# Output weights' low parts pinned on GpSimd, a tanh in a PSUM bank and a small square on ScalarE, in the mixer of a two-layer decoder trunk

## The chip, the cores and the metric

The kernel runs on one core of a Trainium2 chip. A core has five engines that each work through their own list of instructions in order and meet only at semaphores: TensorE (PE in the profile; its weight loads are PEld), VectorE (DVE), ScalarE (ACT), GpSimd (POOL) and SyncE (SP), which here only issues DMAs. [...]

The metric is device time in microseconds for one execution. Before the change it is 1792.57 us, the median of 3 runs (1792.52 to 1795.35).

## The reference

Two layers, each a feed-forward block, a mixer and a second feed-forward block, on x of 512 positions by 1024 features. The change touches the mixer alone:

```python
h = rms_norm(x, mix_norm[l])
a, g, q, k, v = jnp.split(h @ w_in[l], splits, axis=-1)
conv_out = conv_module(a, g, conv_w[l], conv_b[l], conv_norm[l])
...
diff_out = diff_attention(q, k, v, rel_bias, lam, lam_init, subln_norm[l])
x = x + jnp.concatenate([conv_out, diff_out], axis=-1) @ w_out[l]

def conv_module(a, g, conv_w, conv_b, conv_norm):
    u = a * jax.nn.sigmoid(g)
    y = lax.conv_general_dilated(u, rhs, ...) + conv_b      # causal, depthwise, 31 taps
    return jax.nn.silu(rms_norm(y, conv_norm))              # norm over the 512 channels
```

diff_attention has four heads. Each has two softmax maps, A1 - lambda * A2 weighs the values, and the result gets an RMS norm per head.

## The kernel before

All products of weights are made in three matmuls: a float32 weight or activation is split into a high part (a rounding copy, written by ScalarE at L100) and a low part (the difference, L101, by VectorE or GpSimd), and high x high, high x low and low x high are summed in PSUM (`mm3`, L172, L175, L176). `chunk` loads 128 x 1024 weights over the SP queue into one of 5 raw buffers and makes the two parts in one of 4 buffers each. Features stand on partitions and positions on the free axis.

The mixer of a layer goes so. The input projection gives gated conv channels u (4 tiles of 128 channels), then keys, queries and values. `attend(n)` runs a software pipeline over 16 steps, a step being one head of one block of 128 queries, blocks in the order 3, 2, 1, 0: scores on TensorE (L717, two float32 matmuls into banks "sc" and "po"), bias added on VectorE (L721), exp on ScalarE (L725), the two maps joined on VectorE (L728, L730, L731), transposed by TensorE (L738), copied by ScalarE (L740), and multiplied with the values (L747). After a block's fourth head its norm is taken: the squared sums of the exps `se` (L754, VectorE, 128 x 4), squares on ScalarE (L756), a reduction (L758), sum and power on GpSimd (L759, L223), the scaling (L762), a transpose (L774) and the split into high and low parts (L776, L777). Conv and attention write their parts into `acth` and `actl`, conv into feature tiles 0 to 3.

The conv module runs beside attention. Channel tile 0 has its 31 taps on ScalarE and GpSimd (products `prod`, L671, sums `yp`, L672), tiles 1 and 2 on VectorE (L686), tile 3 has 10 taps on the first pair and 21 on VectorE, joined at L689. Squares (L655, L658) are summed on GpSimd (`csum`, L659). `conv_finish` turns them into 1/rms per position: transposes (L230), a reduction and a scaling on VectorE (L234, L235), the power on GpSimd (L223), transposes back (L243) and a copy to `rb` (L247). Then, for each channel tile, GpSimd multiplies with rb (L697), ScalarE takes a tanh into an SBUF buffer of which there is one (L699), VectorE makes (tanh + 1) * z (L700), ScalarE the high part (L701) and VectorE the low part from z and the high part (L702).

The output projection takes the conv half first (`half` 0, all positions, 8 output tiles of 12 matmuls of 512 columns), then the attention half for positions 256 to 511 and 0 to 255 (256 columns). Each pair of output tiles uses one chunk of `wout`, with the low part on GpSimd. Its banks are the score banks "sc" and "po"; VectorE adds each tile to x (L828).

The order of instructions on each engine is made by a scheduler from the program and the estimates it has, except where `keep_in_program_order` pins an instruction against those written before and after it. So the first four chunks of `wout`, written after attention, are in fact loaded early, and their low parts stand among GpSimd's last conv taps.

Of the kernel before, what the change touches and what calls it, by code (L numbers as in the profile page):

```python
# [11 lines left out]
F32 = mybir.dt.float32  # L12
F32R = mybir.dt.float32r
I32 = mybir.dt.int32
AF = mybir.ActivationFunctionType
# [3 lines left out]
P = 128  # L19
DEPTH = 2  # L20
SEQ = 512
# [46 lines left out]
def trunk(ctx: ExitStack, tc: tile.TileContext, xt, par, lamv, relb, onehot,  # L68
# [12 lines left out]
    def f32(ap):  # L81
        return ap.bitcast(F32)
# [3 lines left out]
    def bank(tag, name):  # L86
        return psum.tile([P, 512], F32, tag=tag, name=name, bufs=BANKS[tag])
# [5 lines left out]
        dt = F32 if "raw" in tag else F32R  # L93
        return wp.tile([P, n], dt, tag=tag, name=tag, bufs=RING[tag])

    def parts_of(raw, hi, lo, eng=None, first=False):
        if first:
            V.tensor_scalar(hi, raw, 1.0, None, op0=ALU.mult)
        else:
            S.activation(hi, raw, AF.Copy)  # L100
        (eng or V).tensor_tensor(out=lo, in0=raw, in1=f32(hi), op=ALU.subtract)  # L101

    def chunk(src, eng=None):
        raw, hi, lo = ring("wraw"), ring("whi"), ring("wlo")
        nc.sync.dma_start(raw, src)
        parts_of(raw, hi, lo, eng)
        return hi, lo

    def by_halves(src):
# [435 lines left out]
    def mixer(l, pr, after):  # L545
        with tc.tile_pool(name="mix", bufs=1) as mp, tc.tile_pool(name="mt", bufs=2) as mt:
# [111 lines left out]
                    S.activation(sq, y, AF.Square)  # L658
                    G.tensor_tensor(csum, csum, sq, op=ALU.add)  # L659

            def conv_taps(c, n):

                wc = _AT["conv_w"] + c * TAPS
                yp = None
                if n:
                    yp = mp.tile([P, SEQ], F32, tag="yp%d" % (n < TAPS), name="yp")
                    G.tensor_scalar(yp, us[c][:, 0:SEQ], pars[l][:, wc : wc + 1], col(l, "conv_b", c),
                                    op0=ALU.mult, op1=ALU.add)
                    for t in range(1, n):
                        p = mt.tile([P, SEQ], F32, tag="prod", name="prod")  # L670
                        S.activation(p, us[c][:, t : t + SEQ], AF.Copy, scale=pars[l][:, wc + t : wc + t + 1])  # L671
                        G.tensor_tensor(yp, yp, p, op=ALU.add)  # L672
                if n == TAPS:
                    ys[c] = yp
                    conv_square(c, yp)
                    return
                y = bank("y", "ps_y")
                if not n:
                    V.tensor_scalar(y, us[c][:, 0:SEQ], pars[l][:, wc : wc + 1], col(l, "conv_b", c),
                                    op0=ALU.mult, op1=ALU.add)  # L680
                else:
                    V.tensor_scalar(y, us[c][:, n : n + SEQ], pars[l][:, wc + n : wc + n + 1], None, op0=ALU.mult)

                ys[c] = us[c][:, PAD:]
                for t in range(n + 1 if n else 1, TAPS):
                    V.scalar_tensor_tensor(ys[c] if t == PAD and not n else y, us[c][:, t : t + SEQ],  # L686
                                           pars[l][:, wc + t : wc + t + 1], y, op0=ALU.mult, op1=ALU.add)
                if n:
                    V.tensor_tensor(ys[c], y, yp, op=ALU.add)  # L689
                conv_square(c, ys[c])  # L690

            def conv_finish():
                rcv = spread(rows_rstd(csum, CC, "c")[0], "rb")
                for c in range(CT):
                    z = ys[c]
                    hg = ghalf[l][:, c : c + 1]
                    G.tensor_tensor(z, z, rcv, op=ALU.mult)  # L697
                    th = mt.tile([P, SEQ], F32, tag="gl", name="th", bufs=1)
                    S.activation(th, z, AF.Tanh, scale=hg)  # L699
                    V.scalar_tensor_tensor(z, th, 1.0, z, op0=ALU.add, op1=ALU.mult)  # L700
                    S.activation(ch[:, c, :], z, AF.Copy, scale=hg)  # L701
                    V.scalar_tensor_tensor(cl[:, c, :], z, hg, f32(ch[:, c, :]), op0=ALU.mult, op1=ALU.subtract)  # L702
# [40 lines left out]
            def values(i, h):  # L743
                if h == 0:
                    pos[i] = bank("mm", "ps_o")
                for j in range(i + 1):
                    T.matmul(pos[i][:, h * VD : (h + 1) * VD], ats[i, h][:, j * P : (j + 1) * P], vv[:, j, h, :],  # L747
                             start=j == 0, stop=j == i)
                if h < HEADS - 1:
                    return  # L750
                po = pos[i]

                se = small.tile([P, HEADS], F32, tag="se", name="se")
                V.scalar_tensor_tensor(se, sums[i][:, 0, :], VD * EPS, sums[i][:, 0, :], op0=ALU.mult, op1=ALU.mult)  # L754
                sq = tmp.tile([P, SEQ], F32, tag="sq", name="sq")
                S.activation(sq, po, AF.Square)  # L756
                so = small.tile([P, HEADS], F32, tag="so", name="so")
                V.tensor_reduce(so, sq.rearrange("p (h d) -> p h d", h=HEADS), axis=AX.X, op=ALU.add)  # L758
                G.tensor_tensor(so, so, se, op=ALU.add)  # L759
                ro = rsqrt(so, HEADS)  # L760
                ov = mt.tile([P, HEADS, VD], F32, tag="ov", name="ov")
                V.tensor_tensor(  # L762
                    ov, po.rearrange("p (h d) -> p h d", h=HEADS),
                    ro.unsqueeze(2).broadcast_to([P, HEADS, VD]), op=ALU.mult,
                )
                outs[i] = ov
# [39 lines left out]
            for n in range(2):  # L806
                attend(n)
                project_values(NT - 1 - 2 * n)
                project_values(NT - 2 - 2 * n)
            for c in range(CT):  # L810
                conv_taps(c, POOL_TAPS[c])
            for n in range(2, len(steps) + 5):
                attend(n)
            conv_finish()

            for half, t in ((0, slice(0, SEQ)), (1, slice(SEQ // 2, SEQ)), (1, slice(0, SEQ // 2))):
                if t.stop == SEQ:
                    w = [None] * 4  # L820
                for m in range(KT):
                    if w[m // 2] is None:
                        w[m // 2] = chunk(wout[l, half, m // 2], G)
                    ps = bank(("sc", "po")[m % 2], "ps_out")[:, : t.stop - t.start]
                    for kk in range(4):
                        k = half * 4 + kk
                        mm3(ps, wpart(w[m // 2], (m % 2) * 4 + kk), (ch[:, k, t], cl[:, k, t]), kk == 0, kk == 3)
                    V.tensor_tensor(x[:, m, t], ps, x[:, m, t], op=ALU.add)  # L828

                    if half == 1 and t.start == 0 and m < KT // 2:  # L830
                        after(m)
# [12 lines left out]
    for l in range(DEPTH):  # L844
        nxt = {}

        def then(l2, gain):
            def after(m):
                if m == 0:
                    nxt["p"] = Prep(l2, gain)  # L850
                nxt["p"].tile(m)
            return after
# [82 lines left out]
```

## Time and profile before

| What | Value |
|---|---|
| median of 3 runs | 1792.57 us (1792.52 to 1795.35) |
| the profiled execution | 1792.75 us, of which 1791.0 us are its span |
| granted TensorE clock | 1.000 |
| mixer tail of layer 0 (last value projections to the next feed-forward block) | about 471 to 551 us of the span |
| the same of layer 1 | about 889.5 us later |

A page of the profile gives the busy time of each engine and the chain of waits that ended last. A timeline row is: start, duration (us), engine, line, operation, output and inputs, shapes, count; in brackets the idle time before it and what ended that. Rows that merge several instructions give the time from the first's start to the last's end. A group row has the line, operation, shapes and count, then busy us and mean ns, then idle time before. Matmuls overlap, so the issue interval, not the duration, is what one costs.

### The profile page before, as it was taken

How to read it: one execution, taken by the hardware profiler on the slowest of the kernel's cores; microseconds unless marked ns; L12 is line 12 of the kernel's file. 1: busy time of each engine (PE TensorE's matmuls, PEld its weight loads, DVE VectorE, ACT ScalarE, POOL GpSimd, SP SyncE). 2: the span in 40 equal slices, each digit the busy share in tenths (PEclk: the TensorE clock that was granted, in tenths of full speed). 3: DMA queues.
4: the chain of work that ended last, by engine and by line, in shares of the span. 5: the costliest groups of instructions: out<-in, count | busy, mean ns of one | idle time of the engine just before them, and what ended most of it. 6: DMA issues, size and time to landing. Idle time of an engine off the chain costs nothing.

```text
span 1791.0 us, 28372 instructions
## 1 busy us (share of the span) xinstructions
PE 1783.5 (100%) x10861; PEld 1591.8 (89%) x10861; DVE 1203.1 (67%) x1849; ACT 895.0 (50%) x1479; POOL 643.1 (36%) x453
## 2 busy tenths in 40 slices
PE   9999999999999999999999999999999999999999
PEld 7899899888788899899888998998887888998997
DVE  7877476568867767477566665765788587674762
ACT  6455265445845455265433643654558354552651
POOL 2242232269843133133102412312798331322420
PEclk9999999999999999999999999999999999999999
DMA  7366466322212367367333654663231133664651
GB/s 247 107 174 185 112 179 175 119 93 94 71 48 84 94 165 191 104 171 193 102 95 99 169 168 121 174 182 118 71 116 50 48 107 96 169 172 112 182 150 59
DMA packets 111721, 231.24 MB, mean 129 GB/s; under 512 B 12151, under 2 KB 33414, under 8 KB 111584
## 3 DMA queue, kind: packets, MB, share of 16 engines
q1 hardware_dynamic: 91488, 191.93, 33.5%
q0 software_dynamic: 19808, 37.33, 12.5%
q8 instruction: 85, 1.39, 0.3%
q14 instruction: 52, 0.43, 0.1%
q10 hardware_dynamic: 288, 0.16, 0.0%
HBM read 227.26 MB, written 3.42 MB: 129 GB/s over the span
## 4 chain that ended last, share of the span: by engine, by line
PE 95%; DVE 4%; DMA 0%; issue 0%; ACT 0%; SPq 0%; DVEq 0%; ACTq 0%
PE ps_pair L384 38%; PE ps_d L172 9%; PE ps_d L176 9%; PE ps_d L175 9%; PE ps_pair L176 5%; PE ps_pair L175 5%; PE ps_pair L172 5%; PE ps_pair L601 2%; PE ps_pair L600 2%; PE ps_pair L602 2%; PE ps_out L175 1%; PE ps_out L176 1%; PE ps_out L172 1%; PE ps_sc L717 1%; DVE actl L261 1%; PE ps_v L632 1%
## 5 line engine op out<-in xcount | busy, mean ns | idle before, releaser
L100 ACT ACTIVATE whi<-wraw 128x512 fp32r<-128x512 f32 (+2 forms) x600 | 466.0, 801 | 611.3 <-PE ps_pair L384 226.4
L101 DVE TENSOR_TENSOR wlo<-wraw,whi 128x512 fp32r<-128x512 f32 (+2 forms) x557 | 521.6, 959 | 219.6 <-ACT whi L100 214.6
L384 PE MATMUL ps_pair<-acth,wlo 128*128 128x256 f32 x1088 | 308.3, 283 | 0.0
L384 PE MATMUL ps_pair<-actl,whi 128*128 128x256 f32 x1088 | 308.3, 283 | 0.0
L384 PE MATMUL ps_pair<-acth,whi 128*128 128x256 f32 x1088 | 308.3, 283 | 0.0
L175 PE MATMUL ps_d<-hl,whi 128*128 128x512 f32 x704 | 274.3, 390 | 0.0
L176 PE MATMUL ps_d<-hh,wlo 128*128 128x512 f32 x704 | 273.1, 389 | 0.0
L172 PE MATMUL ps_d<-hh,whi 128*128 128x512 f32 x704 | 269.3, 390 | 0.0
L384 PE MATMUL ps_pair<-th,wlo 128*128 128x256 f32 x816 | 231.2, 283 | 0.0
L384 PE MATMUL ps_pair<-tl,whi 128*128 128x256 f32 x816 | 231.1, 283 | 0.0
L384 PE MATMUL ps_pair<-th,whi 128*128 128x256 f32 x816 | 231.1, 283 | 0.0
L150 POOL DMA_DIRECT2D wraw<-in_gu x68 | 81.9, 1204 | 412.9 <-DMA wraw<-in_gu 143.2
L155 POOL TENSOR_TENSOR wraw<-wraw 128x512 f32<-128x512 f32 x68 | 104.9, 1543 | 331.0 <-DMA wraw<-in_gu 239.8
L384 PEld LDWEIGHTS ps_pair<-acth,whi 128*128 128x128 f32 x1088 | 209.1, 192 | 0.3
L384 PEld LDWEIGHTS ps_pair<-actl,whi 128*128 128x128 f32 x1088 | 209.1, 192 | 0.3
L384 PEld LDWEIGHTS ps_pair<-acth,wlo 128*128 128x128 f32 x1088 | 209.1, 192 | 0.0
L484 DVE SCALAR_TENSOR_TENSOR x<-ps_d,x 128x512 f32<-128x512 f32 x96 | 64.8, 689 | 179.0 <-PE ps_d L176 178.7
L175 PE MATMUL ps_pair<-actl,whi 128*128 128x512 f32 x448 | 175.0, 391 | 0.3 <-DVE actl L261 0.2
L176 PE MATMUL ps_pair<-acth,wlo 128*128 128x512 f32 x448 | 174.6, 391 | 0.0
L172 PE MATMUL ps_pair<-acth,whi 128*128 128x512 f32 x448 | 174.0, 393 | 0.2 <-ACT whi L100 0.2
L384 PEld LDWEIGHTS ps_pair<-th,whi 128*128 128x128 f32 x816 | 156.7, 192 | 0.6
L384 PEld LDWEIGHTS ps_pair<-tl,whi 128*128 128x128 f32 x816 | 156.7, 192 | 0.7
(169 smaller groups left out, 3247.1 us busy)
## 6 DMA issues: line engine op xcount, KB each, us to landing
wraw<-in_gu SPq DMA_DIRECT2D x208, 256.0 KB, 4.0
wraw<-in_gu SPq DMA_DIRECT2D x104, 512.0 KB, 3.7
wraw<-in_gu POOLq DMA_DIRECT2D x68, 512.0 KB, 5.7
wraw<-in_wqkv SPq DMA_DIRECT2D x24, 512.0 KB, 3.6
wraw<-in_dn SPq DMA_DIRECT2D x84, 128.0 KB, 3.0
wraw<-in_dn SPq DMA_DIRECT2D x32, 256.0 KB, 3.2
wraw<-in_wag SPq DMA_DIRECT2D x16, 512.0 KB, 3.6
wraw<-in_wout SPq DMA_DIRECT2D x16, 512.0 KB, 3.6
```

The source lines that it names most:

```text
L100: S.activation(hi, raw, AF.Copy)
L101: (eng or V).tensor_tensor(out=lo, in0=raw, in1=f32(hi), op=ALU.subtract)
L150: nc.gpsimd.dma_start(two.rearrange("p (b c) -> p b c", b=2), u[:, h[0]].unsqueeze(1).broadcast_to([P, 2, 512]), accum_op=ALU.add)
L155: G.tensor_tensor(more[:, h[0]], two[:, h[1]], whole[:, h[0]], op=ALU.add)
L172: first = T.matmul(ps, wh, xh, start=start, stop=False)
L175: T.matmul(ps, wh, xl, start=False, stop=False)
L176: T.matmul(ps, wl, xh, start=False, stop=stop)
L384: mm = T.matmul(ps, l, r, start=first and i == j == 0, stop=False, skip_group_check=True)
L484: V.scalar_tensor_tensor(x[:, m, :], ps, 0.5, x[:, m, :], op0=ALU.mult, op1=ALU.add)
L600: T.matmul(ps[n], xh[:, t], wh, start=k == 0, stop=False)
L601: T.matmul(ps[n], xh[:, t], wl, start=False, stop=False)
L602: T.matmul(ps[n], xl[:, t], wh, start=False, stop=k == KT - 1)
```

## The change

Three edits in the mixer. (1) The first four chunks of `wout` are asked for at set places of the program, and their low parts on GpSimd are pinned there: the first after VectorE's taps of the last conv tile, the second after the transposes, reduction and power of the conv norm, the third and fourth after `conv_finish`, which now stands inside the attention loop, after step 8, and not behind it. (2) The tanh is written to the PSUM bank "y" and not to an SBUF buffer. (3) `se` is made by ScalarE as a square with a scale, no longer by VectorE.

```diff
-    def parts_of(raw, hi, lo, eng=None, first=False):
+    def parts_of(raw, hi, lo, eng=None, first=False, pin=False):
...
-        (eng or V).tensor_tensor(out=lo, in0=raw, in1=f32(hi), op=ALU.subtract)
-
-    def chunk(src, eng=None):
+        low = (eng or V).tensor_tensor(out=lo, in0=raw, in1=f32(hi), op=ALU.subtract)
+        if pin:
+            tc.keep_in_program_order(low)
+
+    def chunk(src, eng=None, pin=False):
         raw, hi, lo = ring("wraw"), ring("whi"), ring("wlo")
         nc.sync.dma_start(raw, src)
-        parts_of(raw, hi, lo, eng)
+        parts_of(raw, hi, lo, eng, pin=pin)
         return hi, lo
...
-            def conv_taps(c, n):
+            def conv_taps(c, n, then=None):
...
+                if then is not None:
+                    then()
                 if n:
                     V.tensor_tensor(ys[c], y, yp, op=ALU.add)
                 conv_square(c, ys[c])
 
-            def conv_finish():
-                rcv = spread(rows_rstd(csum, CC, "c")[0], "rb")
+            def conv_finish(rcv):
+                rcv = spread(rcv, "rb")
                 for c in range(CT):
                     z = ys[c]
                     hg = ghalf[l][:, c : c + 1]
                     G.tensor_tensor(z, z, rcv, op=ALU.mult)
-                    th = mt.tile([P, SEQ], F32, tag="gl", name="th", bufs=1)
+                    th = bank("y", "ps_th")
                     S.activation(th, z, AF.Tanh, scale=hg)
...
-                V.scalar_tensor_tensor(se, sums[i][:, 0, :], VD * EPS, sums[i][:, 0, :], op0=ALU.mult, op1=ALU.mult)
+                S.activation(se, sums[i][:, 0, :], AF.Square, scale=math.sqrt(VD * EPS))
...
+            wo = []
+
+            def next_wo():
+                wo.append(chunk(wout[l, 0, len(wo)], G, pin=True))
+
             for c in range(CT):
-                conv_taps(c, POOL_TAPS[c])
+                conv_taps(c, POOL_TAPS[c], next_wo if c == CT - 1 else None)
+            rcv = rows_rstd(csum, CC, "c")[0]
+            next_wo()
             for n in range(2, len(steps) + 5):
                 attend(n)
-            conv_finish()
+                if n == 8:
+                    conv_finish(rcv)
+                    next_wo()
+                    next_wo()
...
-                    w = [None] * 4
+                    w = [None] * 4 if half else wo
```

## The prediction

> **What bounds the kernel now.** I read the busy shares first, then the chain of waits, then busy time by stretch, then the engines' timelines of one mixer. Columns of the stretches: start and end, length, and for PE, PEld, DVE, ACT and POOL the busy us with the count of instructions, then granted clock, DMA share and GB/s.
>
> ```profile
> PE 1783.5 (100%) x10861; PEld 1591.8 (89%) x10861; DVE 1203.1 (67%) x1849; ACT 895.0 (50%) x1479; POOL 643.1 (36%) x453
> PE 95%; DVE 4%; DMA 0%; issue 0%; ACT 0%; SPq 0%; DVEq 0%; ACTq 0%
> 471.40:494.16 22.76, 22.52 (x133) 17.24 (x133) 19.01 (x64) 19.44 (x52) 16.81 (x13) 1.00 0.32 93
> 494.16:510.12 15.96, 15.09 (x85) 11.24 (x84) 15.78 (x58) 14.05 (x41) 7.78 (x8) 1.00 0.00 1
> 510.12:550.70 40.58, 40.58 (x276) 37.58 (x274) 19.68 (x32) 14.71 (x21) 15.91 (x10) 1.00 0.22 66
> 484.20:510.10 25.90, 24.79 (x152) 19.70 (x151) 25.43 (x91) 21.98 (x65) 12.20 (x13) 1.00 0.00 1
> ```
>
> TensorE bounds almost everything, so an edit off it is worth only the empty time it takes out of TensorE. The DVE share of the chain lies in the mixer. There, in the tail of attention (494.16 to 510.12), VectorE is busy 15.78 of 15.96 us: it sets the pace. TensorE's 15.09 overstates its work, because matmul ends are modelled. Its work is counted from issue intervals:
>
> ```profile
> 476.40 1.06 PE L747 MATMUL ps_o<-vv,at 128*128 128x128 f32 x8
> 477.29 1.46 PE L717 MATMUL ps_sc<-kt,qz 128*128 128x384 f32 x4
> 512.50 0.39 PE L175 MATMUL ps_out<-actl,whi 128*128 128x512 f32 x1
> 512.73 0.39 PE L176 MATMUL ps_out<-acth,wlo 128*128 128x512 f32 x1
> 494.16:510.12 15.96, 7.52 (x24) 4.00 (x25) 0.00 (x0) 1.00 0.00 1
> 499.61 0.50 PE L172 MATMUL ps_out<-acth,whi 128*128 128x512 f32 x1
> ```
>
> Eight 128-column passes take 477.29 - 476.40 = 0.89 us, 0.11 each; an output matmul takes 0.23. The fifth row is the same stretch with the output matmuls alone: 24, that is 5.5 us. The other 61 (59 of 128 columns, two score passes of 256 at twice the price) take 7.0. So 12.5 of 15.96 us are used and about 3.5 us per layer are empty: about 1.9 before the first output matmul at 499.61, 1.6 after it. That is the whole prize: 2 layers x 3.5 = 7.0 us. Layer 1 repeats layer 0 about 889.5 us later (the last row of the next fence against its 508.27).
>
> **The change part by part.**
>
> ```profile
> 476.86 0.58 DVE L754 SCALAR_TENSOR_TENSOR se<-sums 128x4 f32<-128x4 f32 x1
> 486.08 0.15 DVE L754 SCALAR_TENSOR_TENSOR se<-sums 128x4 f32<-128x4 f32 x1
> 495.49 0.61 DVE L754 SCALAR_TENSOR_TENSOR se<-sums 128x4 f32<-128x4 f32 x1
> 503.98 0.14 DVE L754 SCALAR_TENSOR_TENSOR se<-sums 128x4 f32<-128x4 f32 x1
> 486.15 0.68 DVE L689 TENSOR_TENSOR u<-ps_y,yp 128x512 f32<-128x512 f32 x1
> 498.07 0.69 DVE L700 SCALAR_TENSOR_TENSOR yp<-th,yp 128x512 f32<-128x512 f32 x1
> 499.86 0.74 DVE L702 SCALAR_TENSOR_TENSOR actl<-yp,ghalf,acth 128x512 fp32r<-128x512 f32 x1
> 508.27 0.74 DVE L702 SCALAR_TENSOR_TENSOR actl<-u,ghalf,acth 128x512 fp32r<-128x512 f32 x1
> 469.15 2.40 POOL L101 TENSOR_TENSOR wlo<-wraw,whi 128x1024 fp32r<-128x1024 f32 x1
> 472.74 4.69 POOL L101 TENSOR_TENSOR wlo<-wraw,whi 128x1024 fp32r<-128x1024 f32 x2
> 478.61 2.38 POOL L101 TENSOR_TENSOR wlo<-wraw,whi 128x1024 fp32r<-128x1024 f32 x1
> 483.90 1.27 POOL L672 TENSOR_TENSOR yp<-yp,prod 128x512 f32<-128x512 f32 x1 [0.33 <-ACT prod L671]
> 494.81 1.27 POOL L697 TENSOR_TENSOR yp<-yp,rb 128x512 f32<-128x512 f32 x1 [1.51 <-ACT rb L247]
> 496.04 3.67 POOL L697 TENSOR_TENSOR u<-u,rb 128x512 f32<-128x512 f32 x3
> 498.15 1.56 POOL L697 TENSOR_TENSOR u<-u,rb 128x512 f32<-128x512 f32 x1
> 1397.73 0.74 DVE L702 SCALAR_TENSOR_TENSOR actl<-u,ghalf,acth 128x512 fp32r<-128x512 f32 x1
> ```
>
> The squares of the sums (L754). Four leave VectorE per layer: 0.58 + 0.15 + 0.61 + 0.14 = 1.5 us. The two long ones end at 476.86 + 0.58 = 477.44 and 495.49 + 0.61 = 496.10, just where a GpSimd instruction ends (472.74 + 4.69 = 477.43; 494.81 + 1.27 = 496.08). So a VectorE instruction with both inputs in SBUF waits for the GpSimd instruction that runs; the first rows of the next fence show the same.
>
> On ScalarE the square has no row. The bounds are the accumulator read (0.20) and the smallest copy (0.27); I take 0.25, four per layer 1.0 us. ScalarE is busy 14.05 of 15.96 in the tail, so the room is there, though little: without it, that microsecond would count.
>
> ```profile
> 125.00 2.36 DVE L101 TENSOR_TENSOR wlo<-wraw,whi 128x1024 fp32r<-128x1024 f32 x1
> 135.08 1.22 DVE L101 TENSOR_TENSOR wlo<-wraw,whi 128x1024 fp32r<-128x1024 f32 x1
> 124.99 1.28 POOL L155 TENSOR_TENSOR wraw<-wraw 128x512 f32<-128x512 f32 x1 [4.64 <-DVE ps_pair L407]
> 126.36 2.17 POOL L156 TENSOR_TENSOR wraw<-wraw 128x512 f32<-128x512 f32 x1
> L699 ACT ACTIVATE th<-u,ghalf 128x512 f32<-128x512 f32 x3 | 2.1, 710 | 0.0
> L725 ACT ACTIVATE e<-e,mn 128x512 f32<-128x512 f32 x4 | 2.9, 714 | 0.0
> L725 ACT ACTIVATE ps_sc<-ps_sc,mn 128x512 f32<-128x512 f32 x4 | 2.6, 647 | 0.0
> L725 ACT ACTIVATION_READ_ACCUMULATOR ps_sc<-ps_sc,mn 128x1 f32 x16 | 3.2, 199 | 0.0
> L740 ACT ACTIVATE at<-ps_at 128x128 f32<-128x128 f32 x4 | 1.1, 274 | 3.9 <-PE ps_at L738 3.9
> wraw<-in_wout SPq DMA_DIRECT2D x16, 512.0 KB, 3.6
> 512.92 1.06 ACT L100 ACTIVATE whi<-wraw 128x1024 fp32r<-128x1024 f32 x1 [2.19 <-PE ps_out L175]
> ```
>
> Tanh in a bank. ScalarE: by the exps in SBUF and in a bank 714 - 647 = 0.07 us each, 0.3 a layer. VectorE: L700 keeps its 0.69 but has one SBUF input left, so it no longer meets GpSimd (at 498.07 it held up the product of 498.15: 1.56 against 3.67 - 1.56 = 2.11 for the other two). Worth nothing on the path: GpSimd had nothing urgent behind. There is one bank as there was one buffer, so the four channels stay in series.
>
> The pinned low parts. Now four of 2.35 to 2.40 us stand among GpSimd's last conv taps (469.15, 472.74, 478.61), so the pool taps end at 483.90 + 1.27 = 485.2 and the norm's products start at 494.81. In the changed order five taps follow each other from 469.15: 5 x 1.28, and some 2 us of waiting for ScalarE's products (two of them are moved ahead of exps), end near 477.5. Then low part 0 (to 479.9), the channel sum (482), the rstd's power (after VectorE's reduction, 486.5), low part 1 (488.9), block 3's norm (490.2), four products (1.27 + 3 x 1.09, to 494.8), low parts 2 and 3 (497.2, 499.6). L689 moves from 486.15 to about 479, where VectorE waits anyway. Conv starts 4 to 5 us sooner.
>
> The first use of low part 1 is the third output tile, after 24 output matmuls, and that of part 3 later still: over 10 us of room. The raw buffers come free later, the last at 499.6 in place of 481; of the SP queue behind them, three half-1 loads (3.6 us each) and the first gate load wait. Half 1's high parts start at 512.92, so 9 us of room remain: nothing.
>
> What that is worth. VectorE's list up to the last conv low part (L702, 508.27) loses the squares (0.7 after 484), L689 (0.6), and what stood ahead of it and now stands behind: a reduction, a scaling and a low part of attention blocks (0.6 + 0.6 + 0.66) and three short ones (0.7). Together 3.9 us, so near 505, and TensorE has output matmuls to put between the last scores: 24 ahead of the last score in the changed order against 14. That fills the 1.6 us after the first output matmul. The 1.9 before it stay nearly whole, for L700 and L702 of channel 0 and L700 of channel 1 (1.9 us) now stand ahead of two heads' maps, against 1.2 taken out there; the order of TensorE puts half a microsecond more ahead of it. Unhindered gain per layer: 2.1 us, bounds 1.6 and 3.5.
>
> What it costs. L702 reads z and the high part, both in SBUF. Now it runs at 499.86 and later, when GpSimd's long work is done. In the changed order channel 0's comes near 495: of the list ahead of 499.86, 4 to 5 us now follow it. That is just where low part 2 begins (494.8), and channel 1's comes about 3.5 us behind. If channel 0's starts just after low part 2, it waits all of it, 2.4 us; half way in, 1.2; just before, it costs nothing itself but part 3 then holds channel 1's for 1.9. Bounds 0.1 and 2.5 us per layer; I take 1.4, the middle of these, since VectorE may well be later than my count. Behind the waiting L702 stand the maps of the next heads, for which TensorE waits: it counts in full.
>
> [...]
>
> Sum. Per layer 2.1 - 1.4 = 0.7 us, both 1.4. The profiled execution took 1792.75 us (span 1791.0 and 1.75 around it), 0.18 above the median of the runs shown. 1792.75 - 1.4 = 1791.3.
>
> **The rivals.**
>
> The gap is filled, nothing collides. L702 falls between GpSimd's instructions or after 499.6. Gain 2.1 per layer: 1788.5; with all empty time gone, 1792.75 - 7.0 = 1785.8. For it: low part 3 ends at 499.6, and a VectorE 2 us later than counted meets only its end. Against it: GpSimd is without a pause from 486 to 500.
>
> Tanh holds ScalarE up. ScalarE works in order, and the first tanh now stands ahead of a copy of maps, an exp and block 3's high part. It waits for the first product with rb (491.5), which stands behind low part 1 and block 3's norm. ScalarE gets there near 490, and VectorE needs the tanh near 492, so a product after 492 decides. If it is later by one low part (2.4 us), all engines wait. With the collision at 2.0 as just before low part 2: 2.1 - 2.0 - 2.4 = -2.3 per layer, 1797.4, slower. For it: ScalarE's 88% in the tail. Against it: the chain has 0.5 us in hand by my count, and GpSimd's waits are short.
>
> The moved work changes nothing. TensorE waits for the same heads' maps; what conv wins is lost in VectorE's order: 1792.6. For it: DVE is the bound both ways.
>
> **How the numbers follow.** Collision with a small gain 0.45 (own range 1789.5 to 1793.5); no collision 0.30; tanh late 0.15; nothing 0.10. A measurement tells 0.2%, 3.6 us, from no change: faster is below 1789.0, slower above 1796.2. Faster: nearly all of the second, a little of the first, 0.30. Slower: the third and a worse collision, 0.17. Same 0.53. The range, 1786.6 to 1796.2, leaves out gains of nearly all the empty time and the late tanh.
>
> **What would show it.** Right: the first product with rb on GpSimd near 490 (was 494.81); L702 of channel 0 or 1 at 1.3 to 3 us in place of 0.74, ending where a low part ends; more than 20 output matmuls before the last score; TensorE's steady run of output matmuls beginning 0.3 to 1.5 us sooner relative to the last value projection. Wrong: L702 at 0.74 throughout (then 1788.5), a tanh preceded by idle ScalarE of over 2 us (1797), or taps that still end after 484.

## The result, and the profile after

The changed kernel takes 1796.43 us (median of 18 runs, 1795.30 to 1797.61) against 1792.68 us before (18 runs, 1792.28 to 1795.35): a ratio of 1.0019, 95% interval 1.0012 to 1.0027, 3.75 us slower: little, but clear of the noise. The prediction was 1791.3 us, 1.4 us faster, with a range that ended at 1796.2. The profiled execution took 1795.45 us, span 1793.7; before it was 1792.75 and 1791.0. Line numbers of the changed kernel: L700 is now L704, L702 L706, L697 L701, L717 L721, L731 L735, L747 L751, L172 L174.

GpSimd first; its timeline in the changed kernel:

```profile
476.31 1.27 POOL L674 TENSOR_TENSOR yp<-yp,prod 128x512 f32<-128x512 f32 x1 [0.52 <-ACT prod L673]
...
490.25 1.28 POOL L701 TENSOR_TENSOR yp<-yp,rb 128x512 f32<-128x512 f32 x1
491.49 3.19 POOL L701 TENSOR_TENSOR u<-u,rb 128x512 f32<-128x512 f32 x3
494.64 5.11 POOL L101 TENSOR_TENSOR wlo<-wraw,whi 128x1024 fp32r<-128x1024 f32 x2
```

The last conv tap ends at 476.31 + 1.27 = 477.58 (forecast 477.5), the first product with rb starts at 490.25 (490.2; 494.81 before), low parts 2 and 3 run from 494.64 to 499.75 (494.8 to 499.6). The forecast order and times of GpSimd are there. VectorE's timeline, L706 of channels 0 and 1:

```profile
495.02 2.52 DVE L706 SCALAR_TENSOR_TENSOR actl<-yp,ghalf,acth 128x512 fp32r<-128x512 f32 x1
...
500.30 0.74 DVE L706 SCALAR_TENSOR_TENSOR actl<-u,ghalf,acth 128x512 fp32r<-128x512 f32 x1
```

Channel 0's L706 lies where the prediction put it. It should end after 0.74 us and ends at 497.54, 1.78 us late and 0.55 us behind the end of low part 2 (494.64 + 2.35 = 496.99). Its row has no wait in front of it, the instruction itself is long: here VectorE and GpSimd meet without a semaphore, which the section on the chip rules out. What TensorE does meanwhile, from its timeline:

```profile
495.53 0.71 PE L751 MATMUL ps_o<-vv,at 128*128 128x128 f32 x4 [0.73 <-ACT at L744]
498.58 0.70 PE L721 MATMUL ps_sc<-kt,qz 128*128 128x256 f32 x2 [2.34 <-DVE e L735]
...
501.48 1.61 PE L751 MATMUL ps_o<-vv,at 128*128 128x128 f32 x8
502.84 0.47 PE L174 MATMUL ps_out<-acth,whi 128*128 128x512 f32 x1
```

The values' matmuls end near 496; the next scores wait 2.34 us for a joined map (L735), which stands on VectorE behind the held L706. After that TensorE is not only late but slow: the eight passes of 501.48 to 502.84 take 1.36 us, where eight took 0.89. Busy time by stretches of 1 us (columns as in the prediction; the third figure from the end is the granted clock):

```profile
497.00:498.00 1.00, 0.00 (x0) 0.00 (x0) 1.00 (x2) 0.38 (x3) 1.00 (x1) 1.00 0.00 0
498.00:499.00 1.00, 0.42 (x2) 0.40 (x3) 1.00 (x4) 0.83 (x2) 1.00 (x1) 1.00 0.55 180
499.00:500.00 1.00, 0.65 (x4) 0.18 (x2) 1.00 (x7) 0.79 (x3) 0.92 (x3) 0.61 0.81 328
500.00:501.00 1.00, 0.96 (x4) 0.96 (x5) 1.00 (x3) 0.90 (x5) 1.00 (x1) 0.50 0.16 33
501.00:502.00 1.00, 1.00 (x7) 1.00 (x6) 1.00 (x6) 0.28 (x1) 0.00 (x0) 0.50 0.68 221
502.00:503.00 1.00, 1.00 (x8) 1.00 (x8) 0.96 (x5) 1.00 (x3) 0.00 (x0) 0.69 0.67 274
```

TensorE is empty from 497 to 498, and from about 499.2 to 502.6, by the shares of 0.61 and 0.69, its granted clock is at a half. Before, it was 1.00 throughout. The two tails as a whole, layer 0 and layer 1:

```profile
494.16:510.12 15.96, 12.50 (x67) 10.47 (x66) 14.89 (x43) 11.69 (x37) 7.96 (x7) 0.89 0.19 67
1383.00:1400.00 17.00, 13.54 (x79) 11.62 (x78) 16.82 (x54) 13.51 (x42) 8.86 (x7) 0.90 0.21 64
```

In layer 0 the clock was 1.00 in this stretch before; now it is 0.89, and 0.90 in layer 1. The profiled executions of this study reach the mixer's first score matmul up to 0.9 us apart (456.42 us in e3, 457.32 in e9), so a place in the mixer is counted here from it (456.87 us before, 456.75 changed). From there, the first output matmul comes after 46.09 us, and after 42.74 before: 3.35 us later. Of that, 1.5 us are left when the second feed-forward block begins, as the table in the next section shows.

### The profile page after: what moved, and what is told of

Its sections match the earlier page's. It is cut to its first block, busy times and chain, and to the rows that moved or that the text cites. A ratio compares the mean times of both kernels' runs of the same rounds, so it can differ in the third digit from the quotient of the medians.

```text
span 1793.7 us, 28345 instructions
## 1 busy us (share of the span) xinstructions
PE 1781.1 (99%) x10861; PEld 1593.1 (89%) x10861; DVE 1201.6 (67%) x1841; ACT 895.0 (50%) x1487; POOL 643.2 (36%) x453
## 4 chain that ended last, share of the span: by engine, by line
PE 96%; DVE 3%; issue 0%; DMA 0%; ACT 0%; SPq 0%; DVEq 0%
PE ps_pair L386 38%; PE ps_d L178 9%; PE ps_d L177 9%; PE ps_d L174 9%; PE ps_pair L177 5%; PE ps_pair L178 5%; PE ps_pair L174 5%; PE ps_sc L721 2%; PE ps_pair L602 2%; PE ps_pair L604 2%; PE ps_pair L603 2%; PE ps_out L178 1%; PE ps_out L174 1%; PE ps_out L177 1%; DVE actl L263 1%; PE ps_v L634 1%
## 5 line engine op out<-in xcount | busy, mean ns | idle before, releaser
L174 PE MATMUL ps_d<-hh,whi 128*128 128x512 f32 x704 | 269.1, 389 | 0.0
L174 PE MATMUL ps_pair<-acth,whi 128*128 128x512 f32 x448 | 173.9, 392 | 0.6 <-ACT whi L100 0.6
```

What stands on the lines that cost most here:

```text
L174: first = T.matmul(ps, wh, xh, start=start, stop=False)
```

## The experiments

The time of a run is a median of 5 to 18 executions, with the ratio to the kernel before on the same chip. The chips differ a little (1792.68 to 1793.05 us for the kernel before), so differences between rows are good to about 0.4 us. "FFN 0" is the start of the first matmul of the second feed-forward block of layer 0; "mixer 0" is the time from the first score matmul of layer 0 to there, free of the difference at the start; "layer 1" is the time from FFN 0 to the same point of layer 1. The three are of the profiled execution.

| Kernel | us | ratio, 95% interval | FFN 0 | mixer 0 | layer 1 |
|---|---|---|---|---|---|
| before | 1792.68 | | 550.70 | 93.83 | 889.46 |
| changed | 1796.43 | 1.0019 (1.0012 to 1.0027) | 552.05 | 95.30 | 890.84 |
| e9 collision of channel 0 out | 1792.29 | 0.9996 (0.9987 to 1.0005) | 550.73 | 93.41 | 889.07 |
| e6 collision of channel 0 out, same order | 1792.27 | 0.9997 (0.9988 to 1.0007) | 550.48 | 93.46 | 889.62 |
| e3 low parts 2 and 3 later | 1793.33 | 1.0004 (0.9995 to 1.0013) | 550.23 | 93.81 | 891.13 |
| e1 dummy matmuls | 1794.35 | 1.0009 (1.0000 to 1.0018) | 552.37 | 95.46 | 890.21 |
| e4 pins alone | 1803.88 | 1.0062 (1.0050 to 1.0075) | 555.74 | 99.23 | 894.69 |
| e8 tanh in SBUF | 1801.65 | 1.0050 (1.0037 to 1.0063) | 554.67 | 97.93 | 893.84 |
| e7 small edits alone | 1792.07 | 0.9998 (0.9989 to 1.0007) | 550.52 | 93.56 | 889.27 |
| e2 channel 0 in the bank | 1789.91 | 0.9985 (0.9976 to 0.9994) | 549.40 | 92.45 | 888.12 |
| e12 e2's order, collision | 1798.51 | 1.0029 (1.0018 to 1.0039) | 553.94 | 96.67 | 892.05 |
| e10 all channels in the bank | 1791.71 | 0.9992 (0.9983 to 1.0001) | 550.48 | 93.21 | 888.88 |
| e11 e2 and e3 | 1792.91 | 1.0002 (0.9993 to 1.0010) | 550.97 | 93.83 | 889.51 |
| e13 low part of channel 0 pinned | 1794.30 | 1.0010 (1.0001 to 1.0019) | 550.79 | 94.25 | 889.97 |

### Is the collision the loss?

e3 moves low parts 2 and 3 on GpSimd:

```diff
                 if n == 8:
                     conv_finish(rcv)
+                if n == 10:
                     next_wo()
                     next_wo()
```

e6 leaves the order and gives L706 of channel 0 another operand, a finished bank of attention, as the edit below shows. e9 does the same with the first 128 columns of step 11's score bank, read four times over, the instruction being written behind attend(11). Both leave out channel 0's true low part:

```diff
-                    V.scalar_tensor_tensor(cl[:, c, :], z, hg, f32(ch[:, c, :]), op0=ALU.mult, op1=ALU.subtract)
+                    V.scalar_tensor_tensor(cl[:, c, :], z if c else pos[3], hg, f32(ch[:, c, :]), op0=ALU.mult, op1=ALU.subtract)
```

> Low parts 2 and 3 are asked for two steps later, so they stand on GpSimd behind block 2's sum and power and not right behind the four products. VectorE's order up to and past L706 of channel 0 is the same. Theory: L706 of channel 0 takes 0.74 us, the gap of TensorE and the half clock are gone in this place, and the time is 1789 to 1792; if the low parts then meet L706 of a later channel, 1 to 2.4 us of VectorE are lost there, but with output matmuls at hand TensorE loses less than 1 us of it. Rival, the order costs and not the collision: above 1794.5.

> L706 of channel 0 reads a finished bank of attention in place of z, so channel 0's low part of the conv output is wrong; the order of all engines' instructions is that of the changed kernel, one by one. Only the collision is taken out. Theory (wait and clock together): L706 of channel 0 at 0.75 us in place of 2.52, TensorE's granted clock 1.00 in both layers' tails, 1.8 us of wait and 1 to 1.5 us of clock back per layer: 1789.5 to 1791. Rival, the wait without the clock: 1792.8. Rival, the order itself costs: above 1794.5. The first experiments leave room for part of the last, since with the low parts moved and no collision the time was 1793.3.

> As e6, but the bank that L706 of channel 0 reads in z's place is that of a score of step 11, which no matmul has to wait for (in e6 the values' matmuls waited 1.1 us for the bank it read); channel 0's low part is wrong again. All of layer 0 stands in the order of the changed kernel, and layer 1 up to the end of the same stretch; what follows there is ordered a little differently. Theory (wait and clock): the second feed-forward block of layer 0 begins at 548.8 to 549.4, against 552.05 changed and 550.70 before, and the time is 1789.5 to 1791. Rival, the wait alone: 550.2 and 1792.8. Rival, the order itself costs what the collision seemed to: 550.5 or later, as in e6 (550.48) and e3 (550.23), time 1792 to 1793.5.

In layer 0, e6 has the changed kernel's order on every engine, and e9 too but for two score matmuls of 128 columns, which come four value matmuls later on TensorE. The profile shows no matmul of e9 that waits for the bank that the edit reads. The view of e9's line for channel 0's L706 (minimum, median and maximum in ns; first and last start):

```profile
L833 DVE SCALAR_TENSOR_TENSOR actl<-ps_sc,ghalf,acth x2: 743/745/747, 495.6 to 1384.6; 128x512 fp32r<-128x512 f32 x2
```

TensorE's timeline at the first output matmul:

```profile
501.56 0.50 PE L174 MATMUL ps_out<-acth,whi 128*128 128x512 f32 x1 [0.25 <-DVE mn L726]
```

The stretch of the tail:

```profile
494.16:510.12 15.96, 13.76 (x79) 11.19 (x78) 15.22 (x51) 12.35 (x39) 8.54 (x8) 1.00 0.23 67
```

And on VectorE's timeline channel 1's low part, which is L706 of the changed kernel:

```profile
499.24 1.19 DVE L707 SCALAR_TENSOR_TENSOR actl<-u,ghalf,acth 128x512 fp32r<-128x512 f32 x1
```

With one SBUF input (ps_sc is a PSUM bank) the instruction takes 0.745 us, the clock is 1.00, and the time falls from 1796.4 to 1792.3. So the collision of channel 0, with all that follows from it, costs 4.1 us (4.5 if each kernel is taken from the kernel before on its own chip), 2.1 per layer; the profiled executions have 1.9 in mixer 0 and 1.8 in layer 1. e6 says the same (1792.27), though its values' matmuls wait 1.1 us for the bank that the edit reads. But neither comes near the 1789.5 to 1791 that my theory asked for. Without this collision the new order is 0.4 us per layer faster than the old one (93.41 against 93.83, 889.07 against 889.46), and not 2.1. That is the rival "the order itself costs what the collision seemed to", and the larger part of the miss.

One reservation: e9 and e6 are not free of collisions. Channel 1's low part takes 1.19 us in e9 and 1.21 in e6 in place of 0.74. By estimate it meets the end of low part 3 on GpSimd: in e2, whose first score matmul is 0.37 us earlier, that part ends at 494.84 + 4.67 = 499.51, so in e9 near 499.88, and 499.24 + 1.19 = 500.43 is 0.55 behind it, as L706 of channel 0 was behind low part 2. At most these 0.45 us per layer could be added to the 0.4; no run took them out in this order. e3 (1793.3) settles less than it seems to: L706 of channel 0 took 0.74 to 0.75 us there and the clock was 1.00, but channel 2's took 0.99, mixer 0 took as long as before (93.81), and layer 1 took 1.7 us longer than before, for a reason that was not looked for. It missed its 1789 to 1792.

### How much of it is the clock?

e1 puts four dummy matmuls into the empty stretch.

```diff
+                if n == 11:
+                    for _ in range(4):
+                        tc.keep_in_program_order(T.matmul(pos[steps[n - 3][0]][:, 3 * VD :], ident, ident, start=True, stop=True))
```

> Four dummy float32 matmuls of 128 columns (ident by ident, into columns of a bank that are written anew later) are pinned on TensorE in front of the two score passes of 256 columns that wait in the changed kernel; all else in layer 0 keeps its order. A dummy is four passes of 0.11 us, so four fill 1.8 us of the stretch in which TensorE had nothing from about 495.9 to 498.5. Theory (the collision empties TensorE for over 2 us, and the granted clock then stands at half for 3.2 us): the granted clock of the stretch 494.16 to 510.12 comes back from 0.89 to 1.00, L706 of channel 0 keeps its 2.52 us, and 1.0 to 1.5 us come back per layer: 1793.4 to 1794.4 against 1796.4 of the changed kernel. Rival, the wait alone costs and the clock is of no weight: the dummies only fill a gap, time 1796.0 to 1797.0.

The time is in the range that the theory gave (1793.4 to 1794.4). In the profiled execution the two layers came out differently:

```profile
494.16:510.12 15.96, 13.26 (x74) 11.48 (x73) 14.77 (x44) 11.47 (x36) 7.74 (x7) 0.89 0.22 67
1383.00:1400.00 17.00, 14.27 (x89) 12.06 (x88) 16.54 (x51) 13.35 (x39) 9.68 (x9) 1.00 0.20 65
```

The dummies ran as soon as they could, at 496.24 in layer 0, and filled 0.9 us of the stretch, half of what was expected. This row of TensorE's timeline shows the wait that was left:

```profile
498.75 0.70 PE L721 MATMUL ps_sc<-kt,qz 128*128 128x256 f32 x2 [1.45 <-DVE e L735]
```

In layer 0 the clock still fell (0.89); in layer 1, behind the same wait of 1.45 us, it stayed at 1.00. Layer 1 took 890.21 us where the changed kernel's took 890.84. Over the 11 executions, eight show a clock of 1.000 as a mean of the run, at 1793.81 to 1794.84 us; the three at 0.999 took 1794.87 to 1795.12. The changed kernel's 18 show 0.998 (1795.30 to 1796.39) or 0.997 (1796.21 to 1797.61), so none ran at full clock throughout. By the medians, then, the clock is a good half of the 4.1 us: from 1796.4 to about 1794.1 with the dummies and no fall, and from there to 1792.3 without the wait. By layer 1 of the profiled executions (890.84, 890.21, 889.07) it is 0.6 of 1.8 us, a third. The split is an estimate, since the order behind the tail of layer 1 differs a little.

e5 measures the clock by itself, in one execution; GAPS holds lists of one to twelve widths, the lengths of the VectorE instructions that TensorE waits for.

```diff
+    for rnd in range(3):
+        for cols in GAPS:
...
+            for k in range(56 + 5 * rnd):
+                T.matmul(ps, w, xr, start=True, stop=True)
+            g = ps
+            for c in cols:
+                V.tensor_scalar(gap[:, :c], g[:, :c], 0.5, None, op0=ALU.mult)
+                g = gap
+            V.tensor_tensor(xr, gap, x[:, n % KT, :], op=ALU.add)
```

> Not the trunk: runs of 56 to 66 output-like matmuls (128x512, float32r) stand between waits of set length, each a chain of VectorE instructions of about 0.6 to 7 us; 30 waits, three of each length. The input is handed back as the output. Theory: short waits leave the granted clock at 1.00, waits from about 2.5 us up are followed by a stretch at 0.50; as the wait in the changed kernel lay near that bound, the same length may fall on either side. The stretch at 0.50 is about 3 us whatever the wait's length. Rival (the clock falls for another cause than the wait): the clock stays at 1.00 behind waits of 2.5 to 4 us, or falls behind short ones too.

TensorE's timeline; each row is one run of 56, 61 or 66 matmuls, with the wait before it in brackets:

```profile
29.01 13.03 PE L92 MATMUL ps_run<-xr,w 128*128 128x512 f32 x56 [1.51 <-DVE xr L97]
43.88 14.66 PE L92 MATMUL ps_run<-xr,w 128*128 128x512 f32 x56 [1.84 <-DVE xr L97]
...
410.38 15.29 PE L92 MATMUL ps_run<-xr,w 128*128 128x512 f32 x66 [1.84 <-DVE xr L97]
...
481.05 16.88 PE L92 MATMUL ps_run<-xr,w 128*128 128x512 f32 x66 [2.89 <-DVE xr L97]
501.28 16.89 PE L92 MATMUL ps_run<-xr,w 128*128 128x512 f32 x66 [3.35 <-DVE xr L97]
...
543.63 16.67 PE L92 MATMUL ps_run<-xr,w 128*128 128x512 f32 x66 [4.74 <-DVE xr L97]
```

At full clock 56 take 13.0 us and 66 take 15.3: 0.23 us each, as in the kernel before at a clock of 1.00. Those that take longer, by estimate with a stretch at half clock, take 1.4 to 2.7 us more, mostly 1.6; the mean granted clock of the execution is 0.918. The fall can come after the wait is over: in the changed kernel the wait ends at 498.58, and the clock is 1.00 up to 499 us and falls near 499.2. Of the 29 waits, none of three at 1.51 us was followed by such a longer row, 8 of 15 between 1.84 and 2.90 us were, and all 11 from 3.35 us up. Behind the same wait of 1.84 us the row was longer twice (43.88) and once not (410.38). So in between, the length of the wait alone doesn't decide. The wait of the changed kernel, 2.34 us, lies there, though none of its 18 executions shows a clock of 1.000.

### What are the parts of the change worth?

e4 is the changed kernel with both small edits taken back, e8 with the tanh alone taken back. e7 is the kernel before with both made and no pins.

```diff
-                    th = bank("y", "ps_th")
+                    th = mt.tile([P, SEQ], F32, tag="gl", name="th", bufs=1)
...
-                S.activation(se, sums[i][:, 0, :], AF.Square, scale=math.sqrt(VD * EPS))
+                V.scalar_tensor_tensor(se, sums[i][:, 0, :], VD * EPS, sums[i][:, 0, :], op0=ALU.mult, op1=ALU.mult)
```

> The pinned low parts and the place of the conv norm alone: tanh back in its SBUF buffer, se back on VectorE. Theory: the collision stays as it is, and more instructions with two SBUF inputs stand among GpSimd's work (L704 of four channels, two se of 0.6 us): 1796.4 to 1800. Rival, the squares on ScalarE or the tanh in the bank are what costs: 1791 to 1794, below the changed kernel.

> The changed kernel with the tanh back in its SBUF buffer, in the same order but for one swap of neighbours. By the prediction the bank is worth nothing on the path: 1796 to 1797. Theory now (every VectorE instruction with two SBUF inputs that comes while GpSimd is at long work is held): L704 of channels 0 and 1 meet a product and a low part, 0.9 and 1.7 us more per layer, with a longer stretch at half clock: 1801 to 1804, near the pins alone.

> The kernel before with the two small edits alone: the squares of the sums on ScalarE and the tanh in the bank, nothing pinned. By the prediction, 0.7 us per layer leave VectorE's path for the squares and the tanh is worth nothing: 1790.7 to 1792.7. If the squares or the bank cost anything by themselves, over 1793.5.

L704 of e8, all eight, channels 1 to 3 and then channel 0 (minimum, median and maximum in ns):

```profile
L704 DVE SCALAR_TENSOR_TENSOR u<-th,u x6: 679/684/2436, 498.3 to 1399.7; 128x512 f32<-128x512 f32 x6
L704 DVE SCALAR_TENSOR_TENSOR yp<-th,yp x2: 1574/1574/1574, 492.6 to 1386.2; 128x512 f32<-128x512 f32 x2
```

With the tanh in SBUF L704 has two SBUF inputs: channel 0's takes 1.57 us in both layers and channel 1's up to 2.44, where 0.68 is usual. It takes as long in e4 (1.59 and 2.44 in layer 0), whose timelines show GpSimd beside it: channel 0's (492.88 to 494.47) lies within the products with rb (490.56 to 495.43), and channel 1's ends at 498.61 + 2.44 = 501.05, 0.55 us behind low part 3 (495.39 + 5.11 = 500.50), as L706 ended 0.55 behind low part 2 in the changed kernel. So with the pins the bank is worth 1801.65 - 1796.43 = 5.2 us, and the pins alone cost 11 us (e4, which I had put at 1796.4 to 1800). In both, the granted clock stands at half for 6.8 us in layer 0, twice as long as in the changed kernel (3.4). Without the pins the two edits together give less than can be told (1792.07, interval up to 1.0007).

### Where did the forecast gain go?

e2 leaves channel 0's product in the bank, e10 that of all channels, e11 joins e2 and e3.

```diff
-                    V.scalar_tensor_tensor(z, th, 1.0, z, op0=ALU.add, op1=ALU.mult)
+                    s = th if c == 0 else z
+                    V.scalar_tensor_tensor(s, th, 1.0, z, op0=ALU.add, op1=ALU.mult)
-                    S.activation(ch[:, c, :], z, AF.Copy, scale=hg)
-                    V.scalar_tensor_tensor(cl[:, c, :], z, hg, f32(ch[:, c, :]), op0=ALU.mult, op1=ALU.subtract)
+                    S.activation(ch[:, c, :], s, AF.Copy, scale=hg)
+                    V.scalar_tensor_tensor(cl[:, c, :], s, hg, f32(ch[:, c, :]), op0=ALU.mult, op1=ALU.subtract)
```

> Channel 0's (tanh + 1) * z is left in the PSUM bank of the tanh, so L706 of channel 0 has one SBUF input left. Theory (the collision of this instruction with low part 2 is the loss): it takes 0.7 to 0.8 us in place of 2.52, TensorE has no gap over 1.5 us, the clock stays at 1.00, and the time falls by 1.8 us of waiting and 1 to 1.5 us of clock per layer, from 1796.4 to 1790 (1788.5 to 1791.5). Rival, the wait without the clock: by 1.8 us per layer to 1792.8. Rival, the new order itself costs (conv ahead of the maps, a tanh that holds ScalarE): it stays above 1794.5. The bank is now kept until L706, so the next channel's tanh comes later; this could cost up to 1 us of it.

> (tanh + 1) * z of all four channels is left in the bank, so no L706 has two SBUF inputs; the bank is kept until L706, so the four channels are more in series. Theory: L706 of channels 1 to 3 is at 0.74 us in e2 already, so nothing more is won there, and the longer series costs 0 to 1 us per layer: 1789.5 to 1792, the same as e2 (1789.9) or slower.

> e2 and e3 together: channel 0 in the bank and low parts 2 and 3 two steps later. If collisions are all that the low parts cost, they cost nothing in e2, and moving them gives nothing: 1789.5 to 1791. If the later place brings its own loss by the order that goes with it, as e3 (1793.3) hints: 1791.5 to 1793.5.

e2 is faster than both kernels: 1789.91 us, 0.9985 (0.9976 to 0.9994) of before. It is 2.4 us faster than e9, or 2.0 if each is taken from the kernel before on its own chip; mixer 0 is 0.96 us shorter. Two things differ. None of its eight low parts takes over 0.75 us, so e9's small collision at channel 1 is gone as well. And VectorE has another order: since the bank is kept longer, channel 1's tanh comes later, and the scheduler put two joined maps ahead of channel 1's L704. The next three joins of 256 columns on VectorE (L731 before, L736 in e9 and e2), first before:

```profile
495.09 0.48 DVE L731 SCALAR_TENSOR_TENSOR e<-ps_sc,c,e 128x256 f32<-128x256 f32 x1
...
496.52 0.49 DVE L731 SCALAR_TENSOR_TENSOR e<-ps_sc,c,e 128x256 f32<-128x256 f32 x1
...
499.46 0.49 DVE L731 SCALAR_TENSOR_TENSOR e<-ps_sc,c,e 128x256 f32<-128x256 f32 x1
```

In e9:

```profile
496.85 0.48 DVE L736 SCALAR_TENSOR_TENSOR e<-ps_sc,c,e 128x256 f32<-128x256 f32 x1
...
498.84 0.48 DVE L736 SCALAR_TENSOR_TENSOR e<-ps_sc,c,e 128x256 f32<-128x256 f32 x1
...
501.73 0.48 DVE L736 SCALAR_TENSOR_TENSOR e<-ps_sc,c,e 128x256 f32<-128x256 f32 x1
```

In e2:

```profile
495.92 0.47 DVE L736 SCALAR_TENSOR_TENSOR e<-ps_sc,c,e 128x256 f32<-128x256 f32 x1
...
497.84 0.48 DVE L736 SCALAR_TENSOR_TENSOR e<-ps_sc,c,e 128x256 f32<-128x256 f32 x1
...
499.68 0.48 DVE L736 SCALAR_TENSOR_TENSOR e<-ps_sc,c,e 128x256 f32<-128x256 f32 x1
```

The first score matmul is at 456.87 before, 457.32 in e9 and 456.95 in e2. Counted from there, the join ahead of these three (492.43, 492.45 and 492.08) comes 0.4 us sooner in both new kernels. In e9 the three are then late by 1.3, 1.9 and 1.8 us; in e2 by 0.8, 1.2 and 0.1. The first two stand ahead of e9's small collision, so order alone makes them late. All that TensorE does from the first score matmul to the first output matmul, and from there to FFN 0, is in these two stretches of the kernel before:

```profile
456.87:499.61 42.74, 41.90 (x222) 31.81 (x220) 36.17 (x114) 37.62 (x91) 34.39 (x26) 1.00 0.17 50
499.61:550.70 51.09, 50.82 (x326) 44.96 (x325) 30.16 (x63) 23.35 (x45) 18.90 (x15) 1.00 0.18 52
```

The same in e9:

```profile
457.32:501.56 44.24, 42.04 (x222) 31.88 (x220) 37.91 (x114) 39.85 (x97) 35.72 (x28) 1.00 0.13 38
501.56:550.73 49.17, 49.17 (x324) 45.02 (x325) 28.48 (x59) 21.21 (x43) 17.11 (x13) 1.00 0.22 64
```

Up to the first output matmul both do the same 222 matmuls, shape by shape, so e9's stretch is 1.5 us emptier (44.24 against 42.74); behind it e9 is 1.9 us shorter. The new order fills the second stretch and empties the first.

The last two runs were to test whether that order is enough. e12 is e2 with z in place of s in the last line of its diff, which leaves out channel 0's true low part. e13 takes channel 0's low part out of conv_finish and pins it:

```diff
+                if n == 10:
+                    tc.keep_in_program_order(V.scalar_tensor_tensor(cl[:, 0, :], ys[0], ghalf[l][:, 0:1], f32(ch[:, 0, :]), op0=ALU.mult, op1=ALU.subtract))
```

> As e2, but L706 of channel 0 reads z's old buffer in SBUF (its low part is wrong by that), so the collision is back; VectorE's order up to there and past the next two maps is e2's: two heads' maps stand ahead of L704 of channel 1. Theory (collision and order are two causes that add): the collision costs 3 to 5 us here as in the changed order, so 1793 to 1795, below the changed kernel's 1796.4. Rival, the order of e2 is of no weight and its gain over e9 has another cause (the bank): 1796 to 1797.

> The changed kernel, computing all; L706 of channel 0 is pinned on VectorE behind the last instruction of attention's step 10, so two maps of 256 columns stand ahead of it, and it comes near the end of low part 3. Theory (the maps wait for conv work that is ahead of them, and for the collision): TensorE's first output matmul stays near 500, the collision is below 0.5 us, the clock 1.00, and the time is 1788.5 to 1791. Rival, if the order were of no weight: 1792 to 1793, as e9.

Both missed. In e12 the held instruction on VectorE's timeline:

```profile
495.57 2.48 DVE L707 SCALAR_TENSOR_TENSOR actl<-yp,ghalf,acth 128x512 fp32r<-128x512 f32 x1
```

TensorE's wait behind it:

```profile
498.50 0.70 PE L722 MATMUL ps_sc<-kt,qz 128*128 128x256 f32 x2 [2.20 <-DVE e L736]
```

And the stretches of 1 us in which the granted clock falls and comes back:

```profile
499.00:500.00 1.00, 0.53 (x4) 0.25 (x2) 1.00 (x7) 0.55 (x2) 1.00 (x1) 0.64 0.69 258
...
506.00:507.00 1.00, 1.00 (x7) 0.84 (x6) 0.94 (x3) 1.00 (x5) 0.00 (x0) 0.94 0.00 0
```

The collision takes 8.6 us (e2 to e12) and not 3 to 5. The wait is about the same, 2.20 us against 2.34, but by the shares of 0.64 and 0.94 the clock is at half from 499.3 to 506.1, 6.8 us and twice as long as in the changed kernel; the scores and values in it are short dependent steps (TensorE is busy 0.53 of the microsecond from 499 and of that from 502), and the first output matmul comes at 504.59. The orders behind the first two maps also differ, so this is no clean price; but the theory that collision and order simply add did not hold. In e13 the pinned low part on VectorE's timeline:

```profile
502.78 0.74 DVE L832 SCALAR_TENSOR_TENSOR actl<-yp,ghalf,acth 128x512 fp32r<-128x512 f32 x1
```

TensorE's first two output matmuls:

```profile
500.64 0.48 PE L174 MATMUL ps_out<-acth,whi 128*128 128x512 f32 x1
...
503.60 0.47 PE L177 MATMUL ps_out<-actl,whi 128*128 128x512 f32 x1
```

The maps are early, but the low part is late, and TensorE's order has the second output matmul, the first that reads it, at 503.60, three microseconds after the first; scores, values and transposes of attention stand in between, with waits of their own. The profiled execution (1793.30 us) is also the fastest of the eleven; the two at a granted clock of 0.998 took 1795.28 and 1795.73. Maps ahead of conv work are therefore not enough; that the conv work must also be ready when TensorE runs out of attention is what this trace suggests, and no run tested it. Why e10 and e11 fall behind e2 by 1.8 and 3.0 us was not followed up; in e11 a low part of channels 1 to 3 takes up to 1.35 us against 0.74, which looks like a collision, but what held it was not looked for.

## Why the prediction was wrong, point by point

- TensorE's empty time as the only prize, and GpSimd's new times: right, to 0.2 us where compared.
- The collision: right in place and mechanism. L706 of channel 0 was held 1.78 us, within 0.1 to 2.5, by low part 2. Mis-sized was its price: "it counts in full", 1.4 us. It cost 2.1 us per layer (e9), since the wait was longer than the middle that was taken and the empty stretch that it makes lets the clock fall. No term of the sum had the clock, though it stood at 1.00 in every row quoted.
- The unhindered gain of 2.1 us per layer is the step that failed most. The empty 3.5 us were split wrongly to begin with: from 494.16 to 499.61, 32 passes of 0.11 us and two of 0.22 are 4.0 of 5.45 us, so 1.5 us were empty before the first output matmul, not 1.9, and 2.0 behind it, not 1.6. "That fills the 1.6 us after the first output matmul" held: 24 output matmuls stand ahead of the last score, as forecast, and 1.9 us were won there. "The 1.9 before it stay nearly whole" did not: in e9 the empty time there grew by 1.5. I set 1.9 us of conv instructions ahead of the maps against "1.2 taken out there". Half of these, the joining of channel 3 (L689, 0.6), lay before the join of 492.43, and there e9 is 0.4 ahead; from that join to the next the conv instructions cost 1.7, so the next is late by 1.3. The other half, the square of 495.49, lay behind it, and there a reduction (0.6) and the next score's bias took its place. So without the collision of channel 0 the gain is 0.4 us per layer (1793.05 before on that chip, 1792.29), and, by estimate, at most 0.85 with e9's small collision taken out as well, and not 2.1.
- With the measured terms the sum is 2 x (2.1 - 0.4) = 3.4 us slower; 3.75 was measured, and the difference is that of the kernel before on the two chips. By the prediction's terms it was 2 x (1.4 - 2.1) = 1.4 faster.
- Squares on ScalarE: 0.20 to 0.23 us each against 0.25 taken; no loss seen (e7).
- The tanh in the bank, "worth nothing on the path": wrong with the pins, 5.2 us (e8). I looked at GpSimd's waiting and not at L704's own in the new order.
- The rivals: no tanh held up ScalarE. "The moved work changes nothing" is nearly what the order alone does; the kernel in which truly nothing collides also has another order (e2) and takes 1789.9, where I gave 1788.5.

## What to carry to other kernels

A short instruction that is held up on an engine that feeds TensorE can cost more than its wait (1.78 us held in layer 0, 2.1 lost per layer): look at how long TensorE will be without work, and price a fall of the clock as a chance. In e5 a fall cost mostly 1.6 us, and came behind none of three waits of 1.51 us, 8 of 15 between 1.84 and 2.90, and all 11 from 3.35 up; a stretch at half clock can also last twice as long (6.8 us in e12 against 3.4). Time taken out of an engine's list counts only where the engine is late: count both orders from the same early instruction, since executions start unevenly, find the last place at which they stand nearly level, and count what is put in and taken out from there, not over the whole stage. Where a two-input instruction shares time with long GpSimd work, leaving one input in PSUM removed the collision (2.52 us in the changed kernel, 0.74 in e2) and with the order that came with it made the fastest kernel of this study.

## What the runs showed of the hardware

The clock falls behind shorter waits than the 2.5 us that I had expected for e5, and for equal waits not always: in e5 behind two of three of 1.84 us, and behind 8 of the 15 between 1.84 and 2.90 us. TensorE need not even be wholly idle. In e6, layer 1, its longest wait in the stretch was this, from its timeline:

```profile
1385.31 0.68 PE L751 MATMUL ps_o<-vv,at 128*128 128x128 f32 x4 [1.10 <-DVE actl L706]
```

And yet, in the view by stretches of 1 us:

```profile
1384.00:1385.00 1.00, 0.20 (x2) 0.01 (x1) 1.00 (x3) 1.00 (x3) 1.00 (x2) 1.00 0.00 0
1385.00:1386.00 1.00, 0.68 (x4) 0.52 (x4) 1.00 (x3) 1.00 (x5) 1.00 (x1) 1.00 0.00 0
1386.00:1387.00 1.00, 0.80 (x4) 0.58 (x4) 0.88 (x4) 1.00 (x5) 1.00 (x2) 1.00 0.00 0
1387.00:1388.00 1.00, 0.31 (x3) 0.18 (x2) 1.00 (x7) 1.00 (x3) 1.00 (x1) 0.89 0.73 131
1388.00:1389.00 1.00, 1.00 (x5) 1.00 (x6) 1.00 (x2) 1.00 (x5) 1.00 (x2) 0.50 0.73 299
```

With TensorE busy 0.20, 0.68, 0.80 and 0.31 of four microseconds the clock fell to a half; in layer 0 of the same execution, with 0.07, 0.68, 0.92 and 0.32 (495 to 499 us), it stayed at 1.00. What decides between the two is not shown.
